# First norm of an encoder layer: scaling on ScalarE, offsets in place in PSUM, the residual's rows as one GpSimd block, value projection in two halves

## The chip, the cores and the metric

The kernel runs on one NeuronCore of a Trainium2 chip. Its time is the device time of one execution in microseconds (us); runs of this kernel agree within about 0.2%. TensorE multiplies, VectorE and ScalarE work on rows of 128 partitions, GpSimd does the same more slowly and reads only SBUF, SyncE (SP) issues most of the transfers. The matmuls' results lie in eight banks of PSUM; everything else lies in SBUF.

## The reference

One post-norm encoder layer on x of 1024 tokens by 1024 features, in fp32:

```
x = layer_norm(x, ln_in)
proj = x @ w_in            # columns: qa ka va | qb kb vb | qc kc vc
oa = neighbourhood_attention(qa, ka, va)    # 4 heads on a 16 x 64 grid
ob = sliding_window_gqa(qb, kb, vb)         # 8 heads, band of 128
oc = differential_attention(qc, kc, vc)     # 4 heads, two softmaxes each
x = layer_norm(2**0.25 * x + concat(oa, ob, oc) @ w_out, ln_mix)
x = layer_norm(2**0.25 * x + relu(x @ w_ff1)**2 @ w_ff2, ln_ff)
```

A layer norm is `(x - mean) * rsqrt(var + 1e-5) * g + b` over the 1024 features of a token. The change touches the first norm and what follows it directly: the first projections for the differential attention (`qc`, `kc`, `vc`).

## The kernel before

A product of two fp32 matrices is done as three products of parts: each operand is split into a high part, rounded to the format that TensorE takes (fp32r), and a low part, the rest; `mm3` (lines 141 to 148) adds high x high, high x low and low x high. So every operand needs a copy that rounds ("high", written `hi`) and a subtraction ("low", written `lo`).

The first norm works in two halves of 512 tokens, four tiles of 128 tokens each (`ln_half`). For each tile, mean and variance are taken (`ln_stats` on VectorE, L210; for tile 3 `ln_stats_act`, two ScalarE passes at L216 and L219), GpSimd raises the variance to the power -0.5 (L229), and the tile is scaled in place: tiles 0 and 2 on ScalarE (L250), the other six on VectorE (L252). Then, for each of the eight blocks of 128 features (`dc`), four transposes on TensorE (L258) fill a PSUM tile of tag "t" (two banks), ScalarE applies gain and offset per feature and writes an SBUF buffer (L261), `ln_split` copies the high part (L234 on ScalarE or L236 on VectorE) and subtracts it for the low part (L238). The sixteen results are the transposed x, `xT`, which all projections read.

The normalised tiles themselves are kept for the residual: they are multiplied by a row of gains (L269) and a row of offsets is added (L270), both rows multiplied by 2^0.25 beforehand on GpSimd (L1062), and the result is stored to DRAM (`y1`, L271). Tiles 5 and 7 do this on VectorE, the others on GpSimd.

The program's first part is written in this order (lines 1056 to 1077): the first weights for `qc` and `kc` (`first_w`, high part on ScalarE L350, low part on GpSimd L351), the first half of the norm, the first half of `qc` and `kc` (`feat_pieces`, evicted at L371 and L374/L375 and stored to DRAM), the second half of the norm, the second half of `qc` and `kc`, the bias vector of the attention (`t5_vectors`, a one-hot product, L291), a few scalars, the first table of biases (`toeplitz_c`, a round trip through DRAM), the weights of `vc` (`split_v`, L161 and L163) and the eight token tiles of `vc` (`proj_tok`, evicted at L394 and L133). The weights of `vc` use the same double buffers `whi` and `wlo` as all other projection weights.

Then a loop of 68 steps runs the three attentions; its first 32 steps are the differential one (`c_step`: scores L469, softmax on VectorE L472 and ScalarE L476, the combination of the two softmaxes partly on GpSimd at L483 and L484, transposes L498, values L513). The other projections ("background pieces", such as the second half of the features of `qc` and `kc`) are put into that loop at a lower priority (`run_bg`). After it come the two feed-forward products (L930, L1044).

The order on each engine's queue is not the written one alone: the tile framework plans it once, from modelled times, with the written order as priority (`schedule_with_timeline_sim`). `tc.issue_after(ins)` makes the instructions of its block stand behind `ins` in their queue. Each queue then runs strictly in its planned order, and an instruction waits for its inputs and its buffer.

SBUF buffers used here: 36 "pages" of 4 KB per partition (`page`), four each of two small kinds (`evt`, `evb`). PSUM banks: three "S", two "mm", two "t", one "pv".

Of the kernel before, what the change touches and what calls it, by code (L numbers as in the profile page):

```python
# [39 lines left out]
LN_IN_HI = ("aaaaaaaa", "avavavav")  # L40
LN_IN_LO = ("pvvvvvvv", "vvvvvvvv")
LN_IN_ACT = (0, 2)
LN_IN_ACT_STATS = (3,)
ROWS_VECTOR = (5, 7)
# [36 lines left out]
def encoder_kernel(ctx: ExitStack, tc: tile.TileContext, A: dict, out: bass.AP):  # L81
# [131 lines left out]
    def ln_stats_act(x):  # L213
        scr = sb.tile([P, D], F32, tag="raw", bufs=1, name=nm("raw"))
        s = small([P, 6], "acst", 2)
        nc.scalar.activation(out=scr, in_=x, func=AF.Identity, accum_out=s[:, 0:1])  # L216
        nc.vector.tensor_scalar(out=s[:, 1:2], in0=s[:, 0:1], scalar1=-1.0 / D, scalar2=None, op0=ALU.mult)
        nc.vector.tensor_scalar(out=s[:, 2:3], in0=s[:, 0:1], scalar1=1.0 / D, scalar2=None, op0=ALU.mult)
        nc.scalar.activation(out=scr, in_=x, func=AF.Square, bias=s[:, 1:2], accum_out=s[:, 3:4])  # L219
        nc.vector.tensor_scalar(out=s[:, 4:5], in0=s[:, 3:4], scalar1=1.0 / D, scalar2=EPS, op0=ALU.mult, op1=ALU.add)  # L220
        nc.gpsimd.tensor_tensor(out=s[:, 5:6], in0=s[:, 4:5], in1=pw[:, 0:1], op=ALU.pow)
        return s[:, 2:3], s[:, 5:6]

    def ln_moments(st):
        mv = small([P, 2], "bnmv")
        nc.vector.bn_aggr(out=mv, in_=st)
        ve = small([P, 2], "bnve")
        nc.vector.tensor_scalar(out=ve[:, 0:1], in0=mv[:, 1:2], scalar1=EPS, scalar2=None, op0=ALU.add)  # L228
        nc.gpsimd.tensor_tensor(out=ve[:, 1:2], in0=ve[:, 0:1], in1=pw[:, 0:1], op=ALU.pow)  # L229
        return mv[:, 0:1], ve[:, 1:2]  # L230

    def ln_split(xp, tmp, hi, lo):
        if hi == "a":
            nc.scalar.copy(out=xp[:, 0, :], in_=tmp)  # L234
        else:
            nc.vector.tensor_copy(out=xp[:, 0, :], in_=tmp)  # L236
        eng = nc.vector if lo == "v" else nc.gpsimd
        last_sub[0] = eng.tensor_tensor(out=xp[:, 1, :], in0=tmp, in1=f32(xp[:, 0, :]), op=ALU.subtract)  # L238
# [3 lines left out]
    def ln_half(xs, half, cols, rows, ydram):  # L242

        for j in range(4):
            first = half == 0
            mean, rstd = (ln_stats_act if first and j in LN_IN_ACT_STATS else ln_stats)(xs[j])
            if first and j in LN_IN_ACT:
                nmr = small([P, 1], "nmr", 2)
                nc.vector.scalar_tensor_tensor(out=nmr, in0=mean, scalar=-1.0, in1=rstd, op0=ALU.mult, op1=ALU.mult)
                nc.scalar.activation(out=xs[j], in_=xs[j], func=AF.Identity, scale=rstd, bias=nmr)  # L250
            else:
                nc.vector.tensor_scalar(out=xs[j], in0=xs[j], scalar1=mean, scalar2=rstd,  # L252
                                        op0=ALU.subtract, op1=ALU.mult)
        res = []
        for dc in range(8):
            pt = ps_t()
# [3 lines left out]
            tmp = evt([P, 512])  # L260
            nc.scalar.activation(out=tmp, in_=pt, func=AF.Identity,  # L261
                                 scale=cols[:, 0, dc:dc + 1], bias=cols[:, 1, dc:dc + 1])
            ln_split(xp, tmp, LN_IN_HI[half][dc], LN_IN_LO[half][dc])
            res.append(xp)
        with (tc.issue_after(last_sub[0].ins) if half else ExitStack()):
            for j in range(4):
                t = half * 4 + j
                eng = nc.vector if t in ROWS_VECTOR else nc.gpsimd
                eng.tensor_tensor(out=xs[j], in0=xs[j], in1=rows[0], op=ALU.mult)  # L269
                eng.tensor_tensor(out=xs[j], in0=xs[j], in1=rows[1], op=ALU.add)  # L270
                nc.gpsimd.dma_start(out=ydram[t], in_=xs[j])  # L271
# [1113 lines left out]
```

## Time and profile before

| | us |
|---|---|
| median of three runs | 1223.8 (1222.17 to 1224.81) |
| profiled execution | 1225.86 |
| its span in the trace | 1224.0 |
| busy in the span: TensorE / VectorE / ScalarE / GpSimd | 1148.0 / 990.2 / 642.9 / 415.4 |

The span is what the trace covers; the rest of the execution's time, 1.86 us, lies around it. Busy times are sums over the whole span: an engine with a large sum may still be idle in one stage while another engine is full there. The trace calls the engines PE (TensorE; PEld are its weight loads), DVE (VectorE), ACT (ScalarE) and POOL (GpSimd), and the buffers by the names of the program: `pg` a page, `ev` and `evb` the small buffers, `psm`, `psS`, `pst`, `pspv` the PSUM tiles.

### The profile page before, as it was taken

To read this page: it belongs to the slowest core of one execution; us is meant where nothing else is said; L and a number is where in the kernel's file an instruction comes from. 1 tells how busy PE (TensorE), PEld (TensorE's weight loads), DVE (VectorE), ACT (ScalarE), POOL (GpSimd) and SP (SyncE) were. 2 spreads that over 40 slices of the span, in tenths; PEclk is the share of its full clock that TensorE was granted. 3 is DMA by queue.
4 is the path that set the end of the run, shared out by engine and by line. 5 is a ranking of instruction groups with operands and counts; after the bars stand their busy time and mean duration, and the time that the engine had idled before them with its cause. 6 is when DMAs were issued, how large, how long until landed. Compare 5 with 4: busy or idle time off the path is not lost.

```text
span 1224.0 us, 17025 instructions
## 1 busy us (share of the span) xinstructions
PE 1148.0 (94%) x5642; PEld 949.4 (78%) x5642; DVE 990.2 (81%) x1886; ACT 642.9 (53%) x1239; POOL 415.4 (34%) x363
## 2 busy tenths in 40 slices
PE   4799999999998989988399999999999999999997
PEld 3578879987877867766288888888888888888886
DVE  7855899998666699986897698898684888777995
ACT  5323667766557876655655445455462444444440
POOL 5833556686576766531012122222120000000201
PEclk9889999999999999999599999999999999999999
DMA  7295835363789663324035575664389755255551
GB/s 237 104 303 162 276 127 167 121 166 123 209 228 303 199 164 104 104 86 155 26 129 180 175 244 191 225 230 154 141 318 346 250 178 190 103 187 189 183 163 69
DMA packets 127535, 220.59 MB, mean 180 GB/s; under 512 B 11404, under 2 KB 67628, under 8 KB 127448
## 3 DMA queue, kind: packets, MB, share of 16 engines
q1 hardware_dynamic: 113752, 173.36, 45.3%
q0 software_dynamic: 13696, 46.15, 9.9%
q8 instruction: 45, 0.74, 0.3%
q14 instruction: 42, 0.34, 0.1%
HBM read 152.30 MB, written 74.98 MB: 186 GB/s over the span
## 4 chain that ended last, share of the span: by engine, by line
PE 76%; DVE 12%; issue 5%; DMA 2%; ACT 2%; POOL 1%; SPq 0%; DVEq 0%; POOLq 0%; ACTq 0%
PE psm L147 15%; PE psS L1044 11%; PE psS L930 10%; PE pst L930 7%; PE psm L930 7%; PE pst L1044 5%; PE psm L1044 5%; PE pspv L1044 4%; PE psS L469 2%; PE pspv L513 2%; PE pst L498 2%; PE pst L147 2%; DVE pg L133 2%; DVE pg L238 2%; DVE pg L722 1%
## 5 line engine op out<-in xcount | busy, mean ns | idle before, releaser
L147 PE MATMUL psm<-pg,whi 128*128 128x512 f32 x448 | 150.0, 408 | 7.2 <-DVE pg L238 6.4
L930 PE MATMUL psS<-pg,pg 128*128 128x512 f32 x576 | 135.8, 393 | 9.1 <-ACT pg L827 9.1
L1044 PE MATMUL psS<-pg,pg 128*128 128x512 f32 x576 | 140.5, 389 | 0.0
L229 POOL TENSOR_TENSOR bnve<-bnve,pw 128x1 f32<-128x1 f32 x23 | 21.8, 954 | 335.9 <-DVE bnve L228 335.1
L930 PEld LDWEIGHTS psS<-pg,pg 128*128 128x128 f32 x576 | 109.4, 190 | 32.4 <-ACT pg L827 9.5
L1044 PEld LDWEIGHTS psS<-pg,pg 128*128 128x128 f32 x576 | 108.1, 188 | 22.4
L827 ACT CAST pg<-hr 128x512 fp32r<-128x512 f32 x112 | 69.3, 619 | 97.5 <-PE pst L1044 38.0
L147 PEld LDWEIGHTS psm<-pg,whi 128*128 128x128 f32 x448 | 84.0, 192 | 28.3 <-DVE pg L238 7.3
L476 ACT ACTIVATE pg<-pg,cst 128x1024 f32<-128x1024 f32 x64 | 73.8, 1153 | 57.7 <-DVE cst L472 52.1
L930 PE MATMUL psm<-pg,pg 128*128 128x512 f32 x384 | 89.8, 389 | 0.0
L930 PE MATMUL pst<-pg,pg 128*128 128x512 f32 x384 | 89.6, 389 | 0.0
L147 PE MATMUL psm<-pg,wlo 128*128 128x512 f32 x224 | 89.5, 401 | 0.1
L133 DVE TENSOR_TENSOR pg<-hr,pg 128x512 fp32r<-128x512 f32 x112 | 76.5, 683 | 13.2 <-ACT pg L827 13.1
L133 DVE TENSOR_TENSOR pg<-pst,pg 128x512 fp32r<-128x512 f32 (+2 forms) x112 | 64.5, 589 | 23.8 <-ACT pg L394 15.3
L930 PEld LDWEIGHTS psm<-pg,pg 128*128 128x128 f32 x384 | 72.1, 188 | 14.9
L930 PEld LDWEIGHTS pst<-pg,pg 128*128 128x128 f32 x384 | 72.1, 188 | 14.9
L147 PE MATMUL psm<-whi,pg 128*128 128x256 f32 (+1 forms) x256 | 72.7, 347 | 3.8 <-DVE pg L133 3.7
L938 POOL DMA_DIRECT2D hd<-h x32 | 17.7, 554 | 172.1 <-ACT h L942 172.1
L1044 PE MATMUL psm<-pg,pg 128*128 128x512 f32 x288 | 74.2, 389 | 0.0
L1044 PE MATMUL pst<-pg,pg 128*128 128x512 f32 x288 | 74.2, 389 | 0.0
L133 DVE TENSOR_TENSOR pg<-evb,pg 128x512 fp32r<-128x512 f32 (+1 forms) x112 | 72.7, 658 | 1.7 <-ACT pg L761 1.2
L941 ACT ACTIVATE h<-h 128x512 f32<-128x512 f32 x64 | 40.4, 632 | 62.6 <-DVE h L823 61.6
(214 smaller groups left out, 2818.1 us busy)
## 6 DMA issues: line engine op xcount, KB each, us to landing
hr<-hd SPq DMA_DIRECT2D x28, 1024.0 KB, 6.5
hd<-evb POOLq DMA_DIRECT2D x80, 256.0 KB, 3.2
w1r<-in_w_ff SPq DMA_DIRECT2D x16, 1024.0 KB, 6.1
evb<-in_w_ff SPq DMA_DIRECT2D x64, 256.0 KB, 3.6
qk<-evb SPq DMA_DIRECT2D x52, 256.0 KB, 2.4
y<-pg POOLq DMA_DIRECT2D x24, 512.0 KB, 3.4
pg<-y SPq DMA_DIRECT2D x24, 512.0 KB, 6.7
hd<-h POOLq DMA_DIRECT2D x32, 256.0 KB, 3.6
```

The costliest lines, as they stand in the source:

```text
L133: nc.vector.tensor_tensor(out=o, in0=a, in1=b, op=ALU.subtract)
L147: nc.tensor.matmul(o, a, b, start=(i == 0), stop=(i == n - 1))
L229: nc.gpsimd.tensor_tensor(out=ve[:, 1:2], in0=ve[:, 0:1], in1=pw[:, 0:1], op=ALU.pow)
L238: last_sub[0] = eng.tensor_tensor(out=xp[:, 1, :], in0=tmp, in1=f32(xp[:, 0, :]), op=ALU.subtract)
L469: last_mm[0] = nc.tensor.matmul(sc, q[:, m, (i % 2) * P:(i % 2) * P + P], kst[h][kh][:, m, :], start=True, stop=True)
L476: nc.scalar.activation(out=rt, in_=rt, func=AF.Exp, scale=-1.0, bias=sm[:, m:m + 1], accum_out=sm[:, 2 + m:3 + m])
L498: nc.tensor.transpose(pt[:, kb * P:(kb + 1) * P], src[:, c0:c0 + P], ident)
L513: nc.tensor.matmul(pv[:, 0:256], Vc[h // 2][kb // 4][:, kb % 4, h % 2, :], src[:, kb % 4, :], start=(n == 0), stop=(n == 15))
L827: nc.scalar.copy(out=pg[:, 0], in_=x)
L930: nc.tensor.matmul(o, w[:, e, k], xo[m][k][:, f], start=(n == 0), stop=(n == 11))
L941: nc.scalar.activation(out=dst, in_=dst, func=AF.Relu)
L1044: nc.tensor.matmul(o, h[:, e, sl], w[:, f], start=(k == 0 and n == 0), stop=(k == 15 and n == 2))
```

## The change

- All statistics of the first norm are taken on VectorE; the pair of ScalarE passes for tile 3 is gone.
- All eight tiles are scaled on ScalarE (scale and bias per token, the bias being minus mean times rstd).
- The transposes of even feature blocks go to "S" banks, of odd ones to "t" banks: five banks in all.
- Gain and offset are applied in place in PSUM; copy and subtraction then read PSUM. The high copy is on VectorE for even blocks and on ScalarE for odd ones, the subtraction always on VectorE.
- The residual's rows (the two products with alpha, then a product and a sum for each of the eight tiles) are one block on GpSimd behind the last power of the norm, each tile followed by its store.
- The weights of `vc` are loaded right behind x, and split into pages of their own; their low part is subtracted on VectorE as before.
- The first four token tiles of `vc` come between the two halves of the norm; the bias vector comes ahead of them. The scalars' VectorE part stands behind the second half's subtractions.

```diff
-LN_IN_HI = ("aaaaaaaa", "avavavav")
-LN_IN_LO = ("pvvvvvvv", "vvvvvvvv")
-LN_IN_ACT = (0, 2)
-LN_IN_ACT_STATS = (3,)
-ROWS_VECTOR = (5, 7)
+LN_IN_HI = ("vavavava", "vavavava")
...
-        nc.gpsimd.tensor_tensor(out=ve[:, 1:2], in0=ve[:, 0:1], in1=pw[:, 0:1], op=ALU.pow)
+        last_pow[0] = nc.gpsimd.tensor_tensor(out=ve[:, 1:2], in0=ve[:, 0:1], in1=pw[:, 0:1], op=ALU.pow)
...
-    def ln_half(xs, half, cols, rows, ydram):
+    def ln_half(xs, half, cols):
 
         for j in range(4):
-            first = half == 0
-            mean, rstd = (ln_stats_act if first and j in LN_IN_ACT_STATS else ln_stats)(xs[j])
-            if first and j in LN_IN_ACT:
-                nmr = small([P, 1], "nmr", 2)
-                nc.vector.scalar_tensor_tensor(out=nmr, in0=mean, scalar=-1.0, in1=rstd, op0=ALU.mult, op1=ALU.mult)
+            mean, rstd = ln_stats(xs[j])
+            nmr = small([P, 1], "nmr", 2)
+            nc.vector.scalar_tensor_tensor(out=nmr, in0=mean, scalar=-1.0, in1=rstd, op0=ALU.mult, op1=ALU.mult)
+            with (tc.issue_after(last_sub[0].ins) if half else ExitStack()):
                 nc.scalar.activation(out=xs[j], in_=xs[j], func=AF.Identity, scale=rstd, bias=nmr)
-            else:
-                nc.vector.tensor_scalar(out=xs[j], in0=xs[j], scalar1=mean, scalar2=rstd,
-                                        op0=ALU.subtract, op1=ALU.mult)
         res = []
         for dc in range(8):
-            pt = ps_t()
+            pt = ps_t() if dc % 2 else ps_s()
             for j in range(4):
                 nc.tensor.transpose(pt[:, j * P:(j + 1) * P], xs[j][:, dc * P:(dc + 1) * P], ident)
             xp = page([P, 2, 512], F32R)
-            tmp = evt([P, 512])
-            nc.scalar.activation(out=tmp, in_=pt, func=AF.Identity,
+            nc.scalar.activation(out=pt, in_=pt, func=AF.Identity,
                                  scale=cols[:, 0, dc:dc + 1], bias=cols[:, 1, dc:dc + 1])
-            ln_split(xp, tmp, LN_IN_HI[half][dc], LN_IN_LO[half][dc])
+            if LN_IN_HI[half][dc] == "a":
+                nc.scalar.copy(out=xp[:, 0, :], in_=pt)
+            else:
+                nc.vector.tensor_copy(out=xp[:, 0, :], in_=pt)
+            lo = nc.vector.tensor_tensor(out=xp[:, 1, :], in0=pt, in1=f32(xp[:, 0, :]), op=ALU.subtract)
+            if dc < 5:
+                last_sub[0] = lo
             res.append(xp)
-        with (tc.issue_after(last_sub[0].ins) if half else ExitStack()):
-            for j in range(4):
-                t = half * 4 + j
-                eng = nc.vector if t in ROWS_VECTOR else nc.gpsimd
-                eng.tensor_tensor(out=xs[j], in0=xs[j], in1=rows[0], op=ALU.mult)
-                eng.tensor_tensor(out=xs[j], in0=xs[j], in1=rows[1], op=ALU.add)
-                nc.gpsimd.dma_start(out=ydram[t], in_=xs[j])
         return res
 
+    def ln_rows_out(xs, rows, ydram):
+
+        with tc.issue_after(last_pow[0].ins):
+            for r in rows:
+                nc.gpsimd.tensor_tensor(out=r, in0=r, in1=alpha.broadcast_to([P, D]), op=ALU.mult)
+        for t in range(NT):
+            for k, op in enumerate((ALU.mult, ALU.add)):
+                nc.gpsimd.tensor_tensor(out=xs[t], in0=xs[t], in1=rows[k], op=op)
+            nc.gpsimd.dma_start(out=ydram[t], in_=xs[t])
...
+    def load_vc():
+        raws = [page([P, 4, 256]) for j in range(2)]
+        for j in range(2):
+            load(out=raws[j], in_=w_cols(w_in, VC, 256, 4 * j, 4))
+        return raws
+
+    def split_vc(raws):
+        w = []
+        for raw in raws:
+            hi, lo = page([P, 4, 256], F32R), page([P, 4, 256], F32R)
+            nc.scalar.copy(out=hi, in_=raw)
+            sub(lo, raw, f32(hi))
+            w.append((hi, lo))
+        return w
...
     load_x(range(4, NT))
+    raws_vc = load_vc()
     rows_in = ln_rows("ln_in")
-    for r in rows_in:
-        nc.gpsimd.tensor_tensor(out=r, in0=r, in1=alpha.broadcast_to([P, D]), op=ALU.mult)
-    xT[0] = ln_half(xs[0:4], 0, cols_in, rows_in, y1)
+    xT[0] = ln_half(xs[0:4], 0, cols_in)
     qc[0]()
     kc[0]()
-    xT[1] = ln_half(xs[4:8], 1, cols_in, rows_in, y1)
-    qc[1]()
-    kc[1]()
     t5_vectors()
-    scalars()
-    tabs_c[0] = toeplitz_c(0)
-    wv = split_v(VC, (page([P, 4, 256]), page([P, 4, 256])))
-    for t in range(NT):
+    wv = split_vc(raws_vc)
+
+    def vc(t):
         if t % 4 == 0:
             for hp in range(2):
                 Vc[hp].append(page([P, 4, 2, P], F32R))
         proj_tok(t, wv, [Vc[hp][t // 4][:, t % 4] for hp in range(2)], ps_t())
+
+    for t in range(4):
+        vc(t)
+    xT[1] = ln_half(xs[4:8], 1, cols_in)
+    ln_rows_out(xs, rows_in, y1)
+    qc[1]()
+    kc[1]()
+    with tc.issue_after(last_sub[0].ins):
+        scalars()
+    tabs_c[0] = toeplitz_c(0)
+    for t in range(4, NT):
+        vc(t)
```

## Rows read from the trace of the kernel before

**Rows 1.** Busy time by stretch: PE, PEld, DVE, ACT, POOL, then PEclk, DMA, GB/s.

```profile
20.00:52.00 32.00, 24.84 (x113) 17.54 (x111) 31.93 (x32) 15.06 (x25) 29.50 (x16) 0.99 0.23 69
52.00:70.00 18.00, 15.00 (x48) 9.92 (x49) 13.13 (x14) 6.66 (x11) 8.41 (x8) 0.78 0.60 218
70.00:95.00 25.00, 24.90 (x192) 24.28 (x191) 8.73 (x18) 5.04 (x16) 5.62 (x4) 0.90 1.03 305
95.00:350.00 255.00, 251.19 (x1448) 214.44 (x1448) 217.36 (x531) 159.29 (x291) 156.28 (x96) 1.00 0.59 175
...
160.00:280.00 120.00, 118.22 (x759) 103.90 (x758) 117.15 (x283) 81.30 (x148) 79.69 (x49) 1.00 0.52 151
...
350.00:660.00 310.00, 271.37 (x1377) 219.48 (x1376) 256.23 (x553) 194.67 (x450) 137.92 (x118) 0.95 0.47 145
```

**Rows 2.** Chain of waits in order of time: start us, us, what.

```profile
32.48 8.38 DVE pg L238 x3
...
69.08 8.35 PE pst L147 x46
77.52 15.21 PE pst L147 x132
...
93.88 1.24 DVE wlo L163
...
116.85 3.49 PE psm L147 x15
```

**Rows 3.** Groups by shape, VectorE, 29 to 51 us: busy us, mean ns, idle before.

```profile
L238 DVE TENSOR_TENSOR pg<-ev,pg 128x512 fp32r<-128x512 f32 x5 | 13.9, 2812 | 0.1
L236 DVE CAST pg<-ev 128x512 fp32r<-128x512 f32 x2 | 4.0, 2004 | 0.0
L252 DVE TENSOR_SCALAR pg<-pg,bnmv,bnve 128x1024 f32<-128x1024 f32 x2 | 3.7, 1864 | 0.0
...
L133 DVE TENSOR_TENSOR evb<-psm,evb 128x512 fp32r<-128x512 f32 x1 | 0.7, 674 | 0.0
```

**Rows 4.** The same view, VectorE, 4 to 29.5 us.

```profile
L210 DVE BATCH_NORM_STATS2 bnst<-pg 128x6 f32<-128x512 f32 x14 | 8.7, 667 | 3.9 <-DMA pg<-in_x 3.9
...
L238 DVE TENSOR_TENSOR pg<-ev,pg 128x512 fp32r<-128x512 f32 x5 | 3.3, 681 | 0.0
```

**Rows 5.** The same view, GpSimd, 0 to 95 us.

```profile
L270 POOL TENSOR_TENSOR pg<-pg,pg 128x1024 f32<-128x1024 f32 x6 | 16.5, 2769 | 0.0
...
L271 POOL DMA_DIRECT2D y<-pg x8 | 4.5, 570 | 4.3 <-DVE pg L270 4.3
L1062 POOL TENSOR_TENSOR pg<-pg,alpha 128x1024 f32<-128x1024 f32 x2 | 4.3, 2158 | 0.0
```

**Rows 6.** Timeline: start us, us, engine, line, operation, out<-in, count, idle before.

```profile
8.23 1.06 ACT L216 ACTIVATE raw<-pg 128x1024 f32<-128x1024 f32 x1 [5.99 <-DMA pg<-in_x]
...
10.56 1.82 PE L258 MATMUL pst<-ident,pg 128*128 128x128 f32 x6 [10.56 <-ACT pg L250]
...
19.70 1.20 PE L147 MATMUL psm<-pg,whi 128*128 128x512 f32 x2
...
25.94 2.73 PE L291 MATMUL psS<-onehot,t 32*4 32x512 f32 x6
...
28.60 1.10 PE L258 MATMUL pst<-ident,pg 128*128 128x128 f32 x8
...
52.56 0.41 DVE L236 CAST pg<-ev 128x512 fp32r<-128x512 f32 x1
...
67.38 0.59 ACT L371 CAST evb<-psm 128x512 fp32r<-128x512 f32 x1
...
102.50 0.39 PE L469 MATMUL psS<-pg,ev 128*128 128x512 f32 x1
```

**Rows 7.** Groups by shape, ScalarE, 0 to 95 us.

```profile
L261 ACT ACTIVATE ev<-pst,ln_in_cols 128x512 f32<-128x512 f32 x16 | 12.0, 780 | 19.7 <-PE pst L258 16.8 <-DVE pg L238 2.9
...
L250 ACT ACTIVATE pg<-pg,nmr,bnve 128x1024 f32<-128x1024 f32 x2 | 2.4, 1226 | 0.0
```

More of the change, by code (lines that the diff above doesn't have):

```diff
@@ L211, in ln_stats @@
         return ln_moments(st)
[L213 to L222, printed above, removed]
+    last_pow = [None]
     def ln_moments(st):
@@ L228, in ln_moments @@
         nc.vector.tensor_scalar(out=ve[:, 0:1], in0=mv[:, 1:2], scalar1=EPS, scalar2=None, op0=ALU.add)
-        nc.gpsimd.tensor_tensor(out=ve[:, 1:2], in0=ve[:, 0:1], in1=pw[:, 0:1], op=ALU.pow)
+        last_pow[0] = nc.gpsimd.tensor_tensor(out=ve[:, 1:2], in0=ve[:, 0:1], in1=pw[:, 0:1], op=ALU.pow)
         return mv[:, 0:1], ve[:, 1:2]
-    def ln_split(xp, tmp, hi, lo):
-        if hi == "a":
-            nc.scalar.copy(out=xp[:, 0, :], in_=tmp)
-        else:
-            nc.vector.tensor_copy(out=xp[:, 0, :], in_=tmp)
-        eng = nc.vector if lo == "v" else nc.gpsimd
-        last_sub[0] = eng.tensor_tensor(out=xp[:, 1, :], in0=tmp, in1=f32(xp[:, 0, :]), op=ALU.subtract)
     last_sub = [None]
-    def ln_half(xs, half, cols, rows, ydram):
+    def ln_half(xs, half, cols):
         for j in range(4):
-            first = half == 0
-            mean, rstd = (ln_stats_act if first and j in LN_IN_ACT_STATS else ln_stats)(xs[j])
-            if first and j in LN_IN_ACT:
-                nmr = small([P, 1], "nmr", 2)
-                nc.vector.scalar_tensor_tensor(out=nmr, in0=mean, scalar=-1.0, in1=rstd, op0=ALU.mult, op1=ALU.mult)
+            mean, rstd = ln_stats(xs[j])
+            nmr = small([P, 1], "nmr", 2)
+            nc.vector.scalar_tensor_tensor(out=nmr, in0=mean, scalar=-1.0, in1=rstd, op0=ALU.mult, op1=ALU.mult)
+            with (tc.issue_after(last_sub[0].ins) if half else ExitStack()):
                 nc.scalar.activation(out=xs[j], in_=xs[j], func=AF.Identity, scale=rstd, bias=nmr)
-            else:
-                nc.vector.tensor_scalar(out=xs[j], in0=xs[j], scalar1=mean, scalar2=rstd,
-                                        op0=ALU.subtract, op1=ALU.mult)
         res = []
         for dc in range(8):
-            pt = ps_t()
+            pt = ps_t() if dc % 2 else ps_s()
             for j in range(4):
@@ L380, in feat_pieces, with split_v @@
         return [lambda: piece(0), lambda: piece(1)]
-    def split_v(c0, raws=(None, None)):
-        return [split_w(w_cols(w_in, c0, 256, 4 * j, 4), [P, 4, 256], raw=raws[j], pool=raws[j] is None)
-                for j in range(2)]
+    def split_v(c0):
+        return [split_w(w_cols(w_in, c0, 256, 4 * j, 4), [P, 4, 256], pool=True) for j in range(2)]
+    def load_vc():
[11 more added lines that the diff above has]
+        return w
     def proj_tok(t, ws, dest, pm):
```

## The prediction, written before the changed kernel ran

> **What bounds the kernel now.** I read the busy times by stretch, then the chain of waits, the groups of instructions by shape, and the timeline of the first 105 us. In the stretches [rows 1] the reader should look for the engine that is full. From 20 to 52 us VectorE is busy 31.93 of 32 us while TensorE's 24.84 us hold only 113 products. From 70 to 95 us TensorE is full with 192 products. From 95 to 350 us TensorE is full (251 of 255 us) and VectorE close to it; from 350 to 660 us TensorE idles 38.6 us. So the front, up to about 95 us, is where TensorE starves. The chain of waits [rows 2] says on whom: VectorE, three subtractions of L238 alone taking 8.38 us; then the value projection on TensorE itself from 69.08 to 92.7 us; then VectorE's split of the next weights until 95.12 us.
>
> Why are the subtractions so long? Two groups are to be compared. From 29 to 51 us, where GpSimd hardly stops, the L238 subtraction with both inputs in SBUF takes 2812 ns, the L236 copy 2004 ns and the L252 scaling 1864 ns, but the L133 subtraction that reads PSUM takes 674 ns [rows 3]. Before that stretch the same L238 takes 681 ns [rows 4]. GpSimd's work there is the residual's rows, 2769 ns apiece against 2158 ns for L1062 [rows 5]. So the front is set by VectorE instructions that read SBUF alone while GpSimd reads it too.
>
> **What TensorE needs in the front.** Query and key projections: 96 products of 512 columns at 3.49/15 = 0.233 us [rows 2] are 22.4 us. Value projection: 192 of 256 columns at 15.21/132 = 0.115 us [rows 2] are 22.1 us. 64 transposes at 1.10/8 = 0.14 us [rows 6] are 8.8 us. The bias-vector products are ten passes at (28.60 - 25.94)/6 = 0.44 us [rows 6], 4.4 us. Sum 57.7 us. From 10.56 us (first transpose [rows 6]) to 95.12 us there are 84.6 us, so 26.9 us are waits and slow clock: the ceiling of any gain in the front. The clock shows too: the granted clock is 0.78 of full speed from 52 to 70 us and 0.90 from 70 to 95 us [rows 1], and the first 46 products of the value projection take 8.35 us, 0.18 us each, where the next 132 take 0.115 [rows 2]. TensorE had stood waiting for VectorE just before.
>
> **The change, part by part.**
>
> Start. Today tile 3 of x gets its statistics from two ScalarE passes, and the first product runs at 19.70 us [rows 6]. Now VectorE does all statistics. The tile is there at 8.23 us [rows 6]; two L210 of 0.67 us [rows 4], the small operations and GpSimd's power add about 2.4 us. ScalarE scales four tiles at 1226 ns [rows 7] from about 8.6 us: done at 13.5 us, or some 16 us if the two weight casts, of the same shape, come between. Four transposes (0.5), the offset (0.78 [rows 7]), high copy and subtraction (0.6 to 0.7 each) and handovers follow: first product at 16.4 to 18.5 us. I take 17, 2.7 us earlier.
>
> VectorE. The 16 subtractions now read PSUM and one SBUF page; the nearest row is L133's 674 ns beside a busy GpSimd [rows 3], so 10.9 us, where seven of L238 and L236 alone cost 17.9 us [rows 3]. The eight high copies from PSUM are not shown on VectorE; bounds are 0.41 us, an L236 while GpSimd stood still [rows 6], and 2.0 us, L236 beside it [rows 3]; I take 0.68, as their source is PSUM. Four row operations leave VectorE. Its sum: statistics 10.7, small operations 3.8, copies 5.4, subtractions 10.9, projection outputs and value weights about 11, rest 3: some 45 us in 65. It is no longer the bound; where it is late, five banks instead of two stand in front of it.
>
> The Trainium skill ("SBUF — State Buffer", Who interferes with whom) says that a VectorE instruction with at most one SBUF input and outside its two-port modes does not contend with GpSimd. No row here shows that for a copy from PSUM. By that rule the copy stays near what I took.
>
> ScalarE. It gains six scalings and loses one tile's statistics and four copies: 8 x 1.23 + 16 x 0.78 [rows 7] + 8 x 0.6 + some 13 us of weight casts and outputs = 40 us in 65. An output in place in PSUM is not shown; bounds are 0.59 us, a plain pass of this size [rows 6], and twice today's 0.78; I take 0.78. At 1.56 the 16 offsets would bring ScalarE to 53 us, still under the 65.
>
> The Trainium skill ("ScalarE: Activation LUTs", Rules for kernel authors) speaks against this part: multiplications belong on VectorE, which is faster. This trace agrees only where GpSimd rests; beside it L252 takes 1864 ns against ScalarE's 1226 [rows 3, 7]. By that rule the change would make this step slower; by the rows it is hidden.
>
> GpSimd block. Two products with alpha and 16 row operations, each 2.16 to 2.77 us, and eight stores of 0.57 us [rows 5]: 43 to 54 us, from about 25 us (after the last power) to 68 to 79 us. The attention loop needs GpSimd only after its first scores (102.50 us today [rows 6], some 86 after): hidden; if the block ran past that, the loop's first probability products would wait. Nobody reads its stores in the front. Pages in use then: 8 of x, 2 of rows, 16 of transposed x, 4 of value weights, 4 of values, 34 of 36, so the keys' two still fit.
>
> Value projection in two halves. Its weights (1 MB) are loaded behind x, so SP's row vectors and bias table come after them; the DMA share from 20 to 52 us is 0.23 [rows 1], so I cost this at nothing. Its first 96 products (11 us) need only the first half of x and cover the second half's norm. Its weights no longer hold the buffers that the next weights wait for, so the split of 1.24 us that TensorE waits for at 93.88 us [rows 2] goes too.
>
> **Sum.** From 17 us: 22.4 + 22.1 + 4.4 + 8.8 - 2 (transposes done before) = 55.7, so 72.7 us. Stalls I add: slow clock after the start 3 us (46 x 0.065, as in [rows 2]); the handover to the second half 2 us (a bank's round of 3 us, less transposes into other banks); the value weights' low halves on VectorE beside GpSimd 1 us. The front ends at 78.7 instead of 95.1 us: **16.4 us**. With no stalls and a start at 16.4 it ends at 72.1 (gain 23); with stalls doubled and a start at 18.5 at 86.2 (gain 9). TensorE is full behind it until 350 us [rows 1], so the rest shifts as a block. The profiled execution took 1225.86 us, 1.86 above its span; 1225.86 - 16.4 = 1209.5. The median of the runs is 1223.8, 2.1 below that execution, so I give 1207.4 us.
>
> **Rivals.**
>
> *The keys gate the loop.* The last key output is evicted at 67.38 us, yet the first score runs at 102.50 us [rows 6], 35.1 us later; between them SP issues tables and head loads at a DMA share of 1.03 [rows 1]. After the change the keys are done at about the same time (78.7 less the 11 us of the second value half: 67.7). If the 35 us are a chain of loads, the first score stays near 102.5, TensorE does three or four background pieces early instead, and the loop, where VectorE is busy 117 of 120 us [rows 1], is spared only their VectorE part of about 2 us each: gain 6 to 8, 1217 us. For it: queue in order, DMA full. Against: TensorE did not idle before 102.50, so loads were not shown to be last, and the bias table can now start earlier.
>
> *TensorE never waits:* gain 23 to 26.9, 1199 us. For it: no engine is above 70%. Against: the slow clock at a cold start.
>
> *The re-planned order costs later (slower).* Every queue's order is planned from modelled times, and the planner now starts from another front. The place is 350 to 660 us, where TensorE idles 38.6 us [rows 1] and order decides. It is slower from the point where that idle time grows by 18.8 us; at 25 us it is 8.6 us slower, 1232 us. For it: nothing protects that stretch. Against: the attention steps have a fixed program order and would only shift.
>
> *It does not do what it says:* PSUM gives no shelter, or ScalarE's queue holds offsets behind scalings that wait for a power; the front then ends near 95 us as now, 1223.8.
>
> **Chances.** Forecast (gain 9 to 23) 0.50, keys gate 0.24, never waits 0.08, no change 0.07, slower 0.11. Less than 0.2% (2.4 us) cannot be told from no change here. Faster 0.50 + 0.24 + 0.08 = 0.82; same 0.07; slower 0.11. The range reaches from 1198, in the never-waits case, to 1222, which takes in the keys; it leaves out the slower case, most of no change and little else. The forecast alone spans 1201 to 1215.
>
> **What would show it.** Right: the subtraction near 0.68 us all through the GpSimd block; half of the value projection between the two halves of the norm; its last product near 78 us; the first score near 86; granted clock 1.0 from 50 to 95 us. The keys gate: background products from 78 us on and a first score near 102. Wrong if the subtractions still take above 2 us, if ScalarE is full from 10 to 50 us, or if TensorE's idle time from 350 to 660 us grows.

## The result and the profile after

The changed kernel takes 1213.4 us (1212.95 to 1217.0, four runs) where the kernel before takes 1224.3 us (1222.17 to 1225.03, four runs): ratio 0.992, interval 0.9897 to 0.9943. It is 0.8% faster. The forecast was 1207.4 us, 6 us lower, in a range from 1198 to 1222. The profiled execution took 1213.11 us, its span 1211.3 us, 12.7 us shorter than before.

Line numbers differ in the changed kernel and again in some of the runs below. In the changed kernel L241 is the subtraction (L238 before), L240 the high copy on VectorE, L238 the one on ScalarE, L235 the offset (L261), L228 the scaling (L250), L254 and L255 the rows and stores of the residual (L270, L271), L143 the projection products (L147), L233 the transposes (L258), L466 the first branch's scores (L469), L129 the general subtraction helper (L133), L537 the multiplication of the first branch's output norm (L540).

Busy time by stretch in the changed kernel, with the columns of [rows 1]:

```profile
20.00:52.00 32.00, 32.00 (x182) 24.19 (x182) 18.04 (x33) 17.18 (x28) 27.79 (x16) 1.00 0.64 181
52.00:70.00 18.00, 17.69 (x103) 14.72 (x102) 11.94 (x20) 8.18 (x15) 11.53 (x5) 1.00 0.60 241
70.00:95.00 25.00, 24.35 (x132) 20.79 (x131) 13.42 (x33) 9.35 (x18) 16.82 (x11) 1.00 0.76 248
95.00:350.00 255.00, 248.99 (x1444) 211.68 (x1444) 214.85 (x521) 159.10 (x296) 163.10 (x102) 0.99 0.59 178
350.00:660.00 310.00, 270.48 (x1366) 220.57 (x1365) 260.81 (x549) 196.44 (x447) 128.15 (x116) 0.95 0.45 142
```

Against [rows 1], VectorE falls from 31.93 to 18.04 us of the 32 from 20 to 52 us, and TensorE is full there with 182 matmul instructions (products and transposes) instead of 113. The granted clock is 1.00 in all three stretches of the front (0.99, 0.78, 0.90 before). The record of the clock begins at 21.6 us, though, and before that TensorE runs at about half pace (timeline):

```profile
20.31 0.63 PE L143 MATMUL psm<-pg,wlo 128*128 128x512 f32 x1
20.74 0.63 PE L143 MATMUL psm<-pg,whi 128*128 128x512 f32 x1
...
23.60 0.39 PE L143 MATMUL psm<-pg,wlo 128*128 128x512 f32 x1
23.83 0.39 PE L143 MATMUL psm<-pg,whi 128*128 128x512 f32 x1
```

Two products in a row start 0.43 us apart there, and 0.23 us later on.

VectorE from 13 to 80 us, by shape, with the columns of [rows 3]:

```profile
L241 DVE TENSOR_TENSOR pg<-pst,pg 128x512 fp32r<-128x512 f32 x8 | 5.5, 684 | 2.3 <-ACT pg L238 2.3
L240 DVE CAST pg<-psS 128x512 fp32r<-128x512 f32 x8 | 5.4, 681 | 0.7 <-ACT psS L235 0.7
L241 DVE TENSOR_TENSOR pg<-psS,pg 128x512 fp32r<-128x512 f32 x8 | 5.4, 679 | 0.0
L159 DVE TENSOR_TENSOR wlo<-raw,whi 128x1024 fp32r<-128x1024 f32 x2 | 5.3, 2661 | 7.6 <-ACT whi L157 7.6
...
L129 DVE TENSOR_TENSOR pg<-pg,pg 128x1024 fp32r<-128x1024 f32 x2 | 5.0, 2560 | 0.3 <-ACT pg L378 0.3
```

The subtraction that took 2812 ns takes 679 to 684, the high copy from PSUM 681, though GpSimd works beside them. The four 128x1024 subtractions whose inputs both lie in SBUF (the splits of weights) take 2.6 us; one such split took 1.24 us at 93.88 us in the kernel before [rows 2], while GpSimd stood still.

ScalarE and GpSimd, by shape, from 0 to 80 and 0 to 85 us:

```profile
L228 ACT ACTIVATE pg<-pg,nmr,bnve 128x1024 f32<-128x1024 f32 x8 | 9.7, 1238 | 7.5 <-DVE nmr L226 7.2 <-DMA lq<-in_diff_lam_q 0.3
L235 ACT ACTIVATE psS<-psS,ln_in_cols 128x512 f32<-128x512 f32 x8 | 6.0, 749 | 0.8 <-PE psS L233 0.8
...
L254 POOL TENSOR_TENSOR pg<-pg,pg 128x1024 f32<-128x1024 f32 x16 | 41.6, 2638 | 7.1 <-PE pst L233 7.1
```

The chain of waits of the changed kernel near the end of the front (start us, us, what):

```profile
66.30 2.77 DVE wlo L159
69.06 0.02 issue
69.08 4.36 DMA raw<-in_w_in
...
77.46 3.10 PE pst L143 x24
80.56 0.69 PE psS L466 x3
```

The chain passes through the weight split and a load, yet TensorE waits only 0.8 us from 20 to 80 us, for it has value products to run meanwhile. The last value product starts at 80.3 us and the first score at 80.40 us, 22.1 us earlier than the 102.50 of [rows 6]. The first score alone would flatter the change, for before it the kernel before has run 22 more products of 512 columns (131 against 109).

### The profile page after: what moved, and what is told of

The parts are those of the page before. It is cut to its first block, busy times and chain, and to the rows that moved or that the text cites. A ratio compares the mean times of both kernels' runs of the same rounds, so it can differ in the third digit from the quotient of the medians.

```text
span 1211.3 us, 17072 instructions
## 1 busy us (share of the span) xinstructions
PE 1144.5 (94%) x5642; PEld 947.1 (78%) x5642; DVE 972.8 (80%) x1888; ACT 645.9 (53%) x1237; POOL 420.6 (35%) x366
## 4 chain that ended last, share of the span: by engine, by line
PE 75%; DVE 11%; issue 5%; DMA 4%; ACT 2%; POOL 1%; SPq 0%; DVEq 0%; POOLq 0%; ACTq 0%
PE psm L143 14%; PE psS L1041 11%; PE psS L927 11%; PE psm L927 7%; PE pst L927 7%; PE psm L1041 5%; PE pst L1041 5%; PE pspv L1041 4%; DVE pg L129 2%; PE psS L466 2%; PE pspv L510 2%; PE pst L495 1%; DVE pg L469 1%; PE pst L143 1%; DMA raw<-in_w_in 1%
## 5 line engine op out<-in xcount | busy, mean ns | idle before, releaser
L143 PE MATMUL psm<-pg,whi 128*128 128x512 f32 x448 | 151.7, 403 | 2.0 <-DVE pg L240 1.8
L1041 PEld LDWEIGHTS psS<-pg,pg 128*128 128x128 f32 x576 | 108.1, 188 | 22.4
L143 PEld LDWEIGHTS psm<-pg,whi 128*128 128x128 f32 x448 | 83.2, 190 | 21.6 <-DVE pg L240 2.2
L143 PE MATMUL psm<-pg,wlo 128*128 128x512 f32 x224 | 89.3, 399 | 0.8 <-POOL wlo L159 0.8
L927 PE MATMUL pst<-pg,pg 128*128 128x512 f32 x384 | 89.6, 389 | 0.0
L129 DVE TENSOR_TENSOR pg<-hr,pg 128x512 fp32r<-128x512 f32 x112 | 76.6, 684 | 13.0 <-ACT pg L824 12.9
L129 DVE TENSOR_TENSOR pg<-pst,pg 128x512 fp32r<-128x512 f32 (+2 forms) x112 | 64.8, 588 | 19.2 <-ACT pg L391 8.0
L480 POOL TENSOR_TENSOR pg<-pg,cst 128x704 f32<-128x704 f32 x32 | 49.1, 1533 | 80.6 <-DVE cst L477 54.4
L129 DVE TENSOR_TENSOR pg<-evb,pg 128x512 fp32r<-128x512 f32 (+1 forms) x112 | 75.4, 682 | 1.7 <-ACT pg L758 1.2
L143 PE MATMUL psm<-whi,pg 128*128 128x256 f32 (+1 forms) x256 | 71.4, 346 | 3.2 <-DVE pg L129 3.0
```

The costliest lines, as they stand in the source:

```text
L129: nc.vector.tensor_tensor(out=o, in0=a, in1=b, op=ALU.subtract)
L143: nc.tensor.matmul(o, a, b, start=(i == 0), stop=(i == n - 1))
L480: nc.gpsimd.tensor_tensor(out=R[1][:, a], in0=R[1][:, a], in1=sm[:, 6:7].broadcast_to([P, C_POOL]), op=ALU.mult)
L927: nc.tensor.matmul(o, w[:, e, k], xo[m][k][:, f], start=(n == 0), stop=(n == 11))
L1041: nc.tensor.matmul(o, h[:, e, sl], w[:, f], start=(k == 0 and n == 0), stop=(k == 15 and n == 2))
```

## Where the time came from, and where part of it went

First the front. At 80.4 us the changed kernel has done all value products and 109 products of 512 columns; the kernel before had done all value products and 100 of the others at 95.1 us. Nine more at 0.233 us are 2.1 us, so the lead is 95.1 + 2.1 - 80.4 = **16.8 us**. The span is only 12.7 us shorter. From the first product of the first feed-forward matrix to the end both kernels take the same (573.5 to 1224.0 us before, 560.7 to 1211.3 us after), so some 4 us are lost between 80 and 560 us, in the three attention loops.

The stretch from the first score to the first feed-forward product, before and after (same columns):

```profile
102.50:573.50 471.00, 448.56 (x2513) 374.12 (x2512) 398.28 (x956) 307.32 (x661) 282.16 (x195) 1.00 0.55 165
80.40:560.70 480.30, 454.71 (x2535) 379.48 (x2534) 402.12 (x959) 309.48 (x664) 281.90 (x198) 0.99 0.55 167
```

TensorE idles 22.4 us there before and 25.6 us after. Its granted clock, in slices of 2 us, falls once before (around 540 us) and twice after (342 and 455 us), each time to half of full speed, the lower of its two levels, and 1.7 us of full clock are missing in each fall (the sum over the slices of length by the missing share). Together 3.2 + 1.7 = 4.9 us, which is the loss within a microsecond. One place of the changed kernel, in 5 us stretches (same columns):

```profile
335.00:340.00 5.00, 4.50 (x28) 3.85 (x26) 1.41 (x6) 2.33 (x5) 5.00 (x4) 1.00 0.66 216
340.00:345.00 5.00, 2.86 (x11) 2.69 (x12) 4.68 (x10) 2.12 (x7) 4.26 (x2) 0.74 0.59 167
345.00:350.00 5.00, 5.00 (x28) 4.27 (x27) 1.30 (x4) 1.33 (x3) 1.47 (x1) 0.92 0.93 240
```

Timeline of VectorE and TensorE there (columns as in [rows 6]):

```profile
339.93 2.10 DVE L537 TENSOR_TENSOR pg<-pg,css 128x1024 f32<-128x1024 f32 x1
341.95 0.54 DVE L129 TENSOR_TENSOR pg<-pst,pg 128x384 fp32r<-128x384 f32 x1
...
337.07 0.88 PE L613 MATMUL psS<-pg,pg 128*128 128x384 f32 x4
...
342.64 0.87 PE L633 MATMUL pst<-ident,pg 128*128 128x128 f32 x3 [1.65 <-DVE pg L129]
343.17 1.63 PE L613 MATMUL psS<-pg,pg 128*128 128x384 f32 x4
```

TensorE waits 1.65 us for the subtraction L129, which stands in VectorE's queue behind a multiplication of 2.10 us that nobody is waiting for. TensorE idles 2.14 us of five; behind that the clock falls to the lower level, so that its means over the two stretches are 0.74 and 0.92, and four products of L613 take 1.63 us instead of 0.88. In the kernel before the same multiplication ran at 358.07 us for 2.12 us, and TensorE waited there only 1.0 us, for ScalarE. VectorE's order is another one: four such subtractions (128x384) and 28 instructions of the second loop's softmax (L620) stand ahead of the multiplication there, two and 24 (L617) in the changed kernel.

## Experiments

Theory P: the gain is that VectorE reads PSUM instead of SBUF alone beside GpSimd. Rival O: it is the new order of the front. What was measured, in microseconds (each ratio is to executions of the kernel before that were timed together with the run; landmarks are start times; "behind" is TensorE's idle time from the first score to the first feed-forward product, and the number of falls of its clock there):

| kernel | median | ratio to before, interval | last value product | first score | idle behind, falls |
|---|---|---|---|---|---|
| before | 1224.3 | 1 | 93.8 | 102.5 | 22.4, 1 |
| changed | 1213.4 | 0.992 [0.9897, 0.9943] | 80.3 | 80.4 | 25.6, 2 |
| a_sbuf | 1235.9 | 1.010 [1.0081, 1.0118] | 101.8 | 102.0 | 23.4, 2 |
| b_psum | 1234.3 | 1.0093 [1.0076, 1.011] | 83.5 | 93.3 | 29.9, 6 |
| a_vc_late | 1230.5 | 1.006 [1.0041, 1.0078] | 104.3 | 104.5 | 22.7, 0 |
| a_rows_split | 1214.9 | 0.9933 [0.9917, 0.9949] | 80.6 | 80.7 | 24.4, 2 |
| a_vc_late_lam | 1225.2 | 1.0003 [0.9989, 1.0016] | 97.8 | 97.9 | 22.8, 1 |
| a_two_banks | 1217.9 | 0.9938 [0.9919, 0.9956] | 87.6 | 87.7 | 22.8, 3 |
| a_norm_dve | 1218.7 | 0.9942 [0.9924, 0.9959] | 81.0 | 81.1 | 27.3, 4 |
| a_fill38 | 1219.1 | 0.9945 [0.9923, 0.9966] | 80.3 | 80.4 | 25.1, 5 |
| a_vc_late_rs | 1237.4 | 1.0044 [1.0, 1.0088] | 101.2 | 101.3 | 27.7, 4 |
| a_norm_gp | 1207.5 | 0.9848 [0.983, 0.9865] | 80.9 | 81.1 | 20.2, 1 |
| b_fill38 | 1231.2 | 1.0053 [1.0036, 1.0071] | 92.3 | 101.0 | 24.0, 6 |
| b_norm_gp | 1230.8 | 1.005 [1.0032, 1.0068] | 90.7 | 99.4 | 25.6, 3 |

The last three columns are those of one profiled execution of each kernel. Executions of one kernel differ more than the 0.2% of its first three: over all runs the kernel before took 1220.9 to 1229.0 us, at a mean granted clock of 0.977 to 0.985, and 0.0014 of that is one fall of 1.7 us. So the number of falls varies between executions too, and a difference of one or two falls between two kernels is weak evidence by itself.

**The offset into SBUF instead of PSUM (a_sbuf).**

```diff
-            nc.scalar.activation(out=pt, in_=pt, func=AF.Identity,
+            tmp = evt([P, 512])
+            nc.scalar.activation(out=tmp, in_=pt, func=AF.Identity,
                                  scale=cols[:, 0, dc:dc + 1], bias=cols[:, 1, dc:dc + 1])
+            pt = tmp
```

> The changed kernel, but the offset writes an SBUF buffer (four of them) instead of the PSUM bank, so copy and subtraction read SBUF alone again; all else as changed. Theory P (VectorE instructions with SBUF inputs alone are stretched beside GpSimd, and PSUM inputs shelter them): the second half's eight subtractions take about 2.7 us and its four copies about 2 us while the GpSimd block runs, VectorE gets some 20 us more work in the second half, the first score moves from 80.4 us to 88 to 96 us, total 1222 to 1228 us. Rival O (the gain comes from the new order: value projection in two halves, rows in one block): first score within 2 us of 80.4, total 1213 to 1215 us.

VectorE by shape, 28 to 80 us of that run:

```profile
L243 DVE TENSOR_TENSOR pg<-ev,pg 128x512 fp32r<-128x512 f32 x11 | 23.6, 2174 | 0.1
...
L242 DVE CAST pg<-ev 128x512 fp32r<-128x512 f32 x4 | 6.3, 1564 | 2.7 <-ACT ev L236 2.7
```

And who TensorE waits for, 20 to 102 us (us in total, times, longest):

```profile
PE psm L143 <- DVE pg L243: 12.1, 5, 5.3
```

The written order and the engines are the same; what differs is where the operands of VectorE's copies and subtractions (and of ScalarE's odd copies) lie. The subtraction goes from 0.68 to a mean of 2.17 us, TensorE's waits for it from nothing to 12.1 us, the first score from 80.4 to 102.0, the time from 1213.4 to 1235.9 us. The mean granted clock is 0.89, 0.75 and 0.88 from 20 to 52, 52 to 70 and 70 to 102 us, so a part of the 22 us is the clock that falls around these waits. Both bounds of theory P were passed (first score 88 to 96, total 1222 to 1228 us): the effect is larger than it said. Four SBUF buffers take the place of five banks here; two banks alone (a_two_banks, below) cost a third of this. Without its shelter in PSUM the rest of the change makes the kernel 1% slower. This is the decisive run for theory P.

**The kernel before with that part alone (b_psum):** offsets in place in PSUM, five banks, all subtractions on VectorE.

```diff
-LN_IN_LO = ("pvvvvvvv", "vvvvvvvv")
+LN_IN_LO = ("vvvvvvvv", "vvvvvvvv")
...
-            pt = ps_t()
+            pt = ps_t() if dc % 2 else ps_s()
...
-            tmp = evt([P, 512])
+            tmp = pt
```

> The kernel before with one part of the change alone: offsets in place in PSUM with five banks, all sixteen subtractions on VectorE; scaling, statistics, rows and the order of the value projection as before. Theory P: subtractions at 0.68 us, VectorE no longer full from 20 to 52 us, the last value product at 80 to 86 us instead of 93.9, total 1212 to 1217 us. Rival O: last value product at 90 us or later, total 1221 to 1225 us.

VectorE by shape, 13 to 80 us of that run:

```profile
L238 DVE TENSOR_TENSOR pg<-pst,pg 128x512 fp32r<-128x512 f32 x8 | 5.5, 686 | 2.0 <-ACT pg L234 1.8
L238 DVE TENSOR_TENSOR pg<-psS,pg 128x512 fp32r<-128x512 f32 x8 | 5.4, 684 | 2.8 <-ACT pg L234 2.8
```

The subtractions take 0.68 us here too, and the last value product is at 83.5 us, 10.3 us earlier than before, as theory P has it. Yet the kernel is 0.9% slower, which neither expectation allowed. The loops give it all back: TensorE idles 7.5 us more behind the first score, and its clock falls six times instead of once. That the front is faster and the kernel slower made the loops the open question.

**All value products behind the second half (a_vc_late), and GpSimd's rows half by half (a_rows_split).**

```diff
-    for t in range(4):
-        vc(t)
     xT[1] = ln_half(xs[4:8], 1, cols_in)
...
-    for t in range(4, NT):
+    for t in range(NT):
         vc(t)
```

> The changed kernel with all eight token tiles of the value projection behind the second half of the norm, as before. Theory P: TensorE waits 3 to 6 us between the halves, since the second half's norm is not covered, total 1216 to 1220 us. Rival O: most of the gain goes, total 1221 us or more. If the planner covers the gap with other work: total as changed, 1212 to 1215 us.

> The changed kernel with the residual's rows on GpSimd behind each half of the norm (four tiles each) instead of one block behind the last power. Theory P: where the rows stand does not matter once VectorE reads PSUM, total 1212 to 1215 us. Rival O: powers of the second half stand behind rows of the first in GpSimd's queue, the second half is late by 5 us or more, total 1218 us or more.

The order of the rows makes no difference (1214.9 us). The late value products cost 17 us, but not for the reason that either theory had. Timeline of VectorE and GpSimd in a_vc_late:

```profile
50.36 19.56 DVE L129 TENSOR_TENSOR lam<-lam 128x1 f32<-128x1 f32 x1
69.84 0.68 DVE L241 TENSOR_TENSOR pg<-psS,pg 128x512 fp32r<-128x512 f32 x1
...
50.84 9.26 POOL L254 TENSOR_TENSOR pg<-pg,pg 128x1024 f32<-128x1024 f32 x4
60.05 0.59 POOL L255 DMA_DIRECT2D y<-pg  x1
60.67 9.22 POOL L254 TENSOR_TENSOR pg<-pg,pg 128x1024 f32<-128x1024 f32 x4
69.84 2.15 POOL L255 DMA_DIRECT2D y<-pg  x4
```

One subtraction of a single column, with both inputs in SBUF (0.147 us in the kernel before, where GpSimd stood idle at that moment), lasts 19.56 us. It ends where GpSimd's eight row operations end. Such an instruction is called held below; that GpSimd holds it is inferred from these ends. TensorE waits 18.2 us for what stands behind it, and its clock falls to half of full speed.

**The same with that subtraction on ScalarE (a_vc_late_lam).**

```diff
-        sub(lam[:, 2:3], lam[:, 1:2], lam[:, 0:1])
+        nc.scalar.activation(out=lam[:, 2:3], in_=lam[:, 0:1], func=AF.Identity, scale=-1.0, bias=lam[:, 1:2])
```

> The changed kernel with all value products behind the second half of the norm, and the one-column lambda subtraction moved from VectorE to ScalarE, so that no VectorE instruction with two SBUF inputs stands in the middle of GpSimd's block. Theory S (the 19.56 us of that subtraction were nearly the whole loss of the run with late value products; two halves of the value projection are worth only the cover of the second norm, some 2 to 5 us): last value product at 84 to 90 us, no TensorE idle time near 18 us in the front, total 1213 to 1220 us. Rival H (the halves themselves carry the gain, the subtraction was slow because VectorE was behind anyway): last value product stays at 98 us or later, total 1224 us or more.

The numbers are nearly rival H's (last value product at 97.8 us, not 98 or later; total 1225.2 us), the reason is not: with that one out of the way, the next instruction of the kind was held, the split of the next weights (timeline of VectorE):

```profile
56.47 14.60 DVE L159 TENSOR_TENSOR wlo<-raw,whi 128x1024 fp32r<-128x1024 f32 x1 [4.79 <-ACT whi L157]
```

It ends at 71.07 us; GpSimd's rows end at about 70, and the split alone takes 1.2 us. TensorE waits 10.6 us behind it.

**Late value products with the rows half by half (a_vc_late_rs).** The edit is that of a_vc_late and of a_rows_split together.

> The changed kernel with all value products behind the second half of the norm, and GpSimd's rows issued half by half, each behind its half of the norm, as in the kernel before. Theory S (a GpSimd block without pauses holds up whichever VectorE instruction with two SBUF inputs meets it, and that was the whole loss of the two runs with late value products): no VectorE instruction over 4 us in the front, last value product at 84 to 92 us, total 1213 to 1220 us. Rival H (the order itself carries the gain, held instruction or not): last value product at 96 us or later, total 1222 us or more.

Theory S missed: the one-column subtraction was held again, for 18.86 us in the profiled execution. The ten executions fall into two groups, 1221.4 to 1223.1 us (four) and 1237.2 to 1238.3 us (six), about 16 us apart, near the size of the hold; only the upper group has a profile, so that the lower one is free of it is inferred. What the two halves are worth by themselves was not measured in a run without a hold. The nearest number is this lower group, 8 to 10 us above the changed kernel, and it includes the loops' share.

**Two banks, and six scalings on VectorE (a_two_banks, a_norm_dve).**

```diff
-            pt = ps_t() if dc % 2 else ps_s()
+            pt = ps_t()
```

> The changed kernel with the transposes of the norm in two PSUM banks instead of five; nothing else. Theory S (a bank now is held for offset, high copy and subtraction, some 2.1 us plus handovers, so two banks give a tile about every 1.6 us, 8 tiles in 13 us per half, and TensorE has 3.5 us of products per tile only after the first half): last value product 2 to 6 us later than the 80.3 us of the changed kernel, total 1214 to 1219 us. Rival N (banks are no limit, ScalarE or VectorE paces the tiles anyway): landmarks within 1 us, total within 1211 to 1215 us.

> The changed kernel with six of the eight scalings on VectorE, as in the kernel before (tiles 1, 3 and all of the second half). Theory P (VectorE reading SBUF alone beside the GpSimd block takes 1.9 us, on ScalarE 1.24): the four scalings of the second half take about 1.9 us each if the block runs beside them and 0.6 to 1.2 us if not; VectorE gets 5 to 9 us more work in the front; last value product 0 to 5 us later, total 1212 to 1218 us. Rival M (multiplications belong on VectorE, which is faster): last value product 1 to 3 us earlier, total 1209 to 1213 us.

With two banks the last value product is 7.3 us later, 1.3 us above the expected, and the total 4.5 us longer. By then 116 products of 512 columns have run instead of 109; with these 7 x 0.233 = 1.6 us counted as work done, as in the 16.8 us, the three further banks are worth some 5.6 us of the front. With six scalings on VectorE the front is the same (first score 81.1 us), and the 5 us are lost in the loops (four falls of the clock): rival M is refuted, and theory P holds but for a total 0.7 us above its bound. Its scalings took 0.79 to 0.81 us while GpSimd had hardly more than one-column work and 1.78 and 2.83 us beside its 128x1024 operations. The Trainium skill ("ScalarE: Activation LUTs", Rules for kernel authors) sends multiplications to VectorE as the faster engine, with a factor for bf16; of these fp32 scalings the first numbers agree with it against ScalarE's 1.24 us, the others do not. On neither engine did this step set the front.

**The loops alone (a_fill38, b_fill38): the spacing of background pieces.**

```diff
-FILL_C, FILL_A = 3.4, 6
+FILL_C, FILL_A = 3.8, 6
```

> The changed kernel with the planned spacing of background pieces in the first attention loop 3.8 instead of 3.4, nothing in the front. Theory G (the 4 us that are lost behind the front are a matter of where background pieces stand: the changed kernel ends its first loop 24.8 us earlier, but its second takes 11.2 us longer): front landmarks within 0.5 us of the changed kernel, pieces move from the second loop into the first or back, total moves by 2 to 6 us in either direction, down to 1208 us if the loss is recovered. Rival F (the loss is in the front's tail, loads and conversions that come later): total within 1.5 us of 1213.4.

> The kernel before with the planned spacing of background pieces in the first attention loop 3.8 instead of 3.4. Theory G (what is lost behind the front is a matter of how many times TensorE's clock falls between 300 and 573 us: once in the kernel before, twice in the changed one, four times in the changed one with 3.8): front landmarks within 0.5 us of the kernel before, total 1225 to 1231 us, with two or more falls in that stretch. Rival F (the loop's order is robust, the loss is tied to the changed front): total within 1.5 us of the kernel before and one fall.

The front of the changed kernel is untouched (80.4 us); the loops take 6.6 us more, with five falls of the clock instead of two (the expectation of b_fill38 says four). The kernel before loses 6 to 7 us and has six falls in its profiled execution; its total is 0.2 us above the expected range, and its first score moves by 1.5 us, to 101.0, more than expected. So theory G holds in its main point, that the order of pieces in the loops moves either kernel by about 6 us. That the planner also orders the loops anew when only the front changes is seen at the one place above, where the multiplication stands earlier in VectorE's queue; in the other runs it is only inferred from idle times and falls.

**The waiting multiplication on GpSimd (a_norm_gp; b_norm_gp is the kernel before with it).**

```diff
-        nc.vector.tensor_tensor(out=ov, in0=ov, in1=ss.unsqueeze(2).broadcast_to([P, 16, 64]), op=ALU.mult)
+        nc.gpsimd.tensor_tensor(out=ov, in0=ov, in1=ss.unsqueeze(2).broadcast_to([P, 16, 64]), op=ALU.mult)
```

> The changed kernel with one multiplication of the first branch's output norm (128x1024 by 16 factors, twice) on GpSimd instead of VectorE. In the changed kernel the second of them takes 2.10 us on VectorE at 339.93 us, with the subtraction that TensorE waits for behind it; TensorE idles 2.14 us there and its granted clock falls to 0.74 and 0.92 for 10 us. Theory G (the loss behind the front is TensorE's idle time in those stretches and the clock that falls behind it): first score within 0.5 us of 80.4, no fall of the clock at 340 to 350 us, total 2 to 4 us below the changed kernel, 1209 to 1212 us. Rival F (another wait takes its place): second loop as long as before (84 us), total 1212.5 us or more.

> The kernel before with the same multiplication of the first branch's output norm on GpSimd, as a control to the run of the changed kernel with it (1207.5 us, 17.7 below the kernel before of that call). In the kernel before the second of the two takes 2.12 us on VectorE at 358.07 us, and TensorE waits there for ScalarE for 1.0 us only, with the clock at 1.00. Theory G (only the changed kernel's planned order lets TensorE stand behind this instruction): within 3 us of the kernel before, 1221 to 1227 us, so that the change is worth 15 to 17 us with the multiplication on GpSimd in both. Rival K (the move is worth some 5 us in either kernel, and the loss behind the changed front remains): 1217 to 1220 us, the change worth 10 to 12 us in both.

1207.5 us, 17.7 below the kernel before as timed with it and 5.9 below the changed kernel. The wait is gone as theory G says, but the total is 1.5 us below its range and the first score, at 81.1 us, 0.2 us outside its bound. The place in 5 us stretches:

```profile
335.00:340.00 5.00, 4.01 (x26) 3.46 (x25) 1.95 (x6) 2.77 (x5) 4.89 (x4) 1.00 0.76 259
340.00:345.00 5.00, 5.00 (x28) 4.04 (x29) 3.26 (x10) 2.53 (x7) 5.00 (x3) 1.00 0.84 251
345.00:350.00 5.00, 5.00 (x31) 4.25 (x30) 1.33 (x3) 1.51 (x4) 0.31 (x1) 1.00 0.97 207
```

TensorE is full from 340 to 350 us and the clock stays at 1.00. From 335 to 350 us this saves 1.6 us of idle time and the fall's 1.7 us, some 3 of the 5 us by which the span is shorter (1211.3 to 1206.3); the rest comes from other places. Idle time behind the first score falls from 25.6 to 20.2 us, the falls from two to one. In the kernel before, the same move makes it 0.5% slower: neither expectation held. Its falls go from one to three and its idle time from 22.4 to 25.6 us. So the move is no gain as such: the order around it decides. Of all kernels run, a_norm_gp is the fastest.

## Why the prediction was right, point by point

**The bound.** VectorE's instructions that read SBUF alone beside GpSimd were the front's bound: a_sbuf puts these back and loses 22 us, 12.1 of them in TensorE's waits for the subtraction; b_psum, the kernel before with the offset in PSUM, five banks and all subtractions on VectorE, gains 10.3 us in the front.

**The terms.** The copies from PSUM were taken at 0.68 us and took 0.681. The Trainium skill ("SBUF — State Buffer", Who interferes with whom) says that a VectorE instruction with at most one SBUF input, outside the two-port modes, does not contend with GpSimd. The trace agrees, with these 0.681 us and the subtraction's 0.679 to 0.684 beside GpSimd's block. The offset in place was taken at 0.78 and took 0.746 (743 and 749 ns); the start at 17 us was 17.66. The last rows of the GpSimd block ended at 79.4 us and its last stores at 81.5, 2.5 us past the upper end of the 68 to 79 that were given for both, with a pause of 7 us for TensorE's transposes; that moved nothing in the front.

**The front.** Forecast 16.4 us, measured 16.8, and that close by luck, since several terms were off and cancelled. The last value product ended at 80.6 us, not 78.7. The start was 0.7 us late; 13 background products (3.0 us) ran ahead of it; the work that had been summed took 1.5 us more, by its value products (23.6 us for 192 instead of 22.1). Against that, of the 6 us of stalls less came: the half pace after the start, the slow clock of the prediction, cost 1.6 us instead of 3 (six products and four transposes before 21.6 us), and TensorE idled 1.1 us, not 3, from its first product to the last value product:

```profile
17.66:80.56 62.90, 61.82 (x356) 49.59 (x357) 36.61 (x64) 29.67 (x52) 51.10 (x30) 1.00 0.67 215
```

The end 1.9 us later than forecast is a gain of 14.5 us. It becomes 16.8 us, counted at 80.4 us, by the nine background products that the kernel before has still to do (2.1 us), which the forecast had not provided for. The weight split did not go away: two splits of 2.6 us stand in the chain, but they are covered.

**The rivals.** *Keys gate the loop* is refuted: the first score came 0.1 us after the last value product, not near 102 us. *TensorE never waits* was nearly true of the front from 20 to 80 us (0.8 us of waits), but not of the start, where TensorE waits for its input (first product at 17.66 us) and then runs at half pace. *It does not do what it says* is refuted by the 0.68 us.

**The step that failed** is "TensorE is full behind it until 350 us, so the rest shifts as a block". It was taken as a loss of nothing and measured about 4 us: 16.8 became 12.7, and the median is 6 us above the forecast. The medians differ by 1.8 us less than the spans (10.9 against 12.7), as the profiled execution of before was 1.6 above the median of these runs and that of the changed kernel 0.3 below its own. What took the place of the block is the rival *re-planned order*, with another place and a smaller price: idle time from 350 to 660 us, whose growth was a sign of being wrong, grew by 0.9 us only (38.6 to 39.5, and the same stretch holds later work now), but the wait behind L537 at 340 us and a second fall of the clock were new. Its price turned out to be no constant: the change is worth 10.9 us with the loops as they came out, 12.1 with the spacing 3.8 in both kernels, and 23.3 with the multiplication on GpSimd in both (differences of medians, most of them of kernels timed at different times). The 16.8 us of the front lie between.

**Left open.** Why a held instruction stays held through six to eight GpSimd operations in some runs and is done after 1 to 6 us in others (in the changed kernel 1.31 us for the one-column subtraction and 2.75 us for the split at 66.30 us, both with row operations in sequence beside them; 5.71 us for a split in b_psum). What the two halves of the value projection are worth alone, and what the four row operations and the statistics are worth that changed engines: no run puts these back one by one. What the falls of the clock at 455 us (changed) and 540 us (before) stand behind is open, too.

## What to carry to other kernels

Before a VectorE instruction is moved or made shorter, look where its operands lie and what GpSimd does beside it: reading one operand from PSUM took a subtraction from a mean of 2.17 to 0.68 us here, and the first score 21.6 us forward. Judge an edit of an early stage by the landmarks of that stage as well as by the total, for a planner that starts from another front can give back a quarter of the gain (here), or all of it (b_psum), in stages that the edit does not touch; then look for short waits of TensorE and for the granted clock behind them. An instruction that nobody waits for can be the cause, if it stands in a queue ahead of one that somebody does.

## What was not expected of the hardware

A VectorE subtraction of one column with two SBUF inputs, 0.147 us alone, lasted 19.56 and 18.86 us beside GpSimd operations that follow one another, and a 128x1024 split 14.60 us, each until GpSimd's row operations had ended; the longest subtraction with two SBUF inputs in the front of the kernel before took 2.88 us, about as long as one GpSimd operation (2.77 us [rows 5]). The Trainium skill ("SBUF — State Buffer", Who interferes with whom) describes a lock for a whole instruction; these runs show that the wait can span a series of them. Short waits of TensorE can also be dear in a second way, as at 340 us in the changed kernel: behind 2.14 us of idle time in five the clock fell to its lower level, and 1.7 us of full clock went with it, on top of the idle time (3.4 us for both falls behind the first score, 10.2 us for the five of a_fill38). With that wait gone (a_norm_gp) this fall was gone too.
